# Moving six of seven fast-matrix products of a down-projection in between the blocks of the up-projection

## The chip, the cores and the metric

The kernel runs as one program on one core of a Trainium2 chip. The metric is the device time of one execution in microseconds (us); the time of a kernel is the median of several executions. The core has a matrix engine (TensorE, PE in the profile, with its weight loads shown as PEld), a vector engine (VectorE, DVE), a scalar engine (ScalarE, ACT), a general engine (GpSimd, POOL) and a queue engine (SyncE, SP) that here issues DMA transfers. Results of TensorE go to eight accumulator banks of 128 x 512 floats.

## The reference

A two-layer encoder over 256 tokens of width 2048. Each layer is a token mixer (a state-space mixer, then windowed attention) followed by the MLP below, each with a normalisation in front and a residual add behind. Both layers' MLPs are the place of the change:

```
D_MODEL, SEQ, D_FF = 2048, 256, 8192

def sqrelu_mlp(h, w_up, w_down):
    return jnp.square(jax.nn.relu(h @ w_up)) @ w_down

h = h + sqrelu_mlp(rms_norm(h, mlp_norm[i]), mlp_w_up[i], mlp_w_down[i])
```

All inputs and outputs are float32.

## The kernel before

**Matmuls in split precision.** A float32 matrix is split into a high part, which is its value cast to the reduced float32 format that TensorE takes at full rate, and a low part, the difference. A product of two matrices is then three matmuls: high by high, low by high, high by low. ScalarE makes the high part (a cast, lines 679 and 693 for weights, 917 for activations), VectorE the low one (a subtraction, lines 680, 694 and 918).

**Weights.** `wload` (line 665) takes the next source from the list `wsrc`, issues one transfer of 128 x 2048 floats on SP's queue into the next buffer of the ring of raw weights, and makes the high and low part in the next buffers of two more rings. `wnext` (line 710) keeps one block loaded ahead of the one that it hands out. While the MLP runs, the raw ring has two buffers and the high and low rings three each; the down-projection adds one to each for a part of its time. The engines' orders are made by a scheduler at build time from the order in which the program is written and the dependencies; each engine then runs its list in order, and the ring buffers decide how far the loads run ahead.

**Up-projection.** The 8192 hidden features are computed in 64 blocks of 128 (`up_mm`, line 856). A block is 16 matmuls of 512 columns with the high weights (line 858; the right side holds the activations' high and low parts side by side) and 16 of 256 columns with the low weights (line 860), into one bank. `up_post` (line 862) empties the bank: ScalarE copies one half (865), VectorE adds the other (866) and applies the relu and the row scale (867), ScalarE squares (869) into the hidden array `hT`. It is written behind the next block's matmuls. The up-projection uses the eight banks in turn.

**Down-projection.** It makes two passes (`half`), one per 1024 output columns. A pass goes over 32 k-pairs; a pair is two blocks of 128 hidden features, so 256 rows of the weight. The output of a pass is a 2 x 2 grid of banks (`x1` to `x4`: two token halves by two column halves), and a pair is a 2 x 2 by 2 x 2 block product. `plain` (line 938) computes it as 8 block products, `fast` (line 934) as 7 by Winograd's form of Strassen's scheme, from sums and differences of activation and weight blocks. The seven products go to `p1`, `x1`, `x2`, `q5`, `q6`, `q7`, `x3`; the four banks p1 and q5 to q7 collect over all fast pairs of the pass and are combined and added to the residual by `fold` (line 948). The first pass has nine fast pairs (2, 5, ... 26), the second nine others:

```
FORMS = (("p1", 0, 0, 1), ("x1", 1, 0, 2), ("x2", 6, 0, 0), ("q5", 4, 1, 0),
         ("q6", 5, 1, 1), ("q7", 3, 1, 2), ("x3", 2, 1, 3))   # bank, activation form, weight set, weight block
```

`wload_fast` (line 683) makes the weights of a fast pair: it splits three of the four raw blocks (1536 columns, first set), forms three differences in place (lines 696 to 698) and splits all four (2048 columns, second set). `split` (line 902) does the activations of a pair, one pair ahead of the matmuls: for a plain pair a cast and a subtraction of 512 columns, for a fast one also a copy and the sums of lines 912 to 914 and 896 columns.

`end` (line 960) adds the x banks to the residual. Between the two MLPs lies the attention layer, in front of the first the state-space layer; neither is touched but for scratch memory. On-chip memory is handed out by an arena with fixed boundaries (line 189), where a range keeps one number format until all its tenants are freed.

## Time and profile before

| | |
|---|---|
| time, median of 3 runs (lowest to highest) | 2065.54 us (2063.76 to 2065.96) |
| profiled execution: its own time | 2068.43 us |
| profiled execution: span from first to last instruction | 2066.6 us |
| mean granted TensorE clock | 0.996 |
| transferred | 368.47 MB, mean 178 GB/s |
| MLP 1: up-projection, down-projection | about 385 to 747 us, 747 to 1092 us |
| MLP 2: up-projection, down-projection | about 1380 to 1722 us, 1722 to 2064 us |

How to read the rows shown below: an L number is a line of the kernel before; `x` is a count of instructions; a group's row gives its summed busy time, the mean duration of one in ns, and behind the bar the idle time of the engine just ahead of these instructions with the instruction that ended it (behind the arrow). `slot` is a range of on-chip memory, `bank` an accumulator bank, `in_wdn` the down-projection's weights. Matmuls overlap in the pipe, so the mean duration of one is longer than the time from one to the next.

### The profile page before, as it was taken

What the parts mean: (1) busy time and instruction counts of PE and PEld (TensorE: products, weight loads), DVE (VectorE), ACT (ScalarE), POOL (GpSimd) and SP (SyncE); (2) the same over time, 40 slices, a digit from 0 to 9 for tenths busy, and PEclk for the clock granted to TensorE, in tenths of its full rate; (3) what the DMA queues carried; (4) which work ended last, traced back from release to release, by engine and by line L of the source; (5) the groups of instructions that cost most, each with busy time, mean ns of one, the idle gap of its engine ahead of it and who ended that gap; (6) DMA issues with size and microseconds to landing.
All of it is one profiled execution on the core that took longest, in us unless ns stands there. A gap on an engine that the chain in (4) does not pass through costs nothing.

```text
span 2066.6 us, 33166 instructions
## 1 busy us (share of the span) xinstructions
PE 2002.8 (97%) x13736; PEld 1685.1 (82%) x13736; DVE 1478.7 (72%) x2184; ACT 1091.4 (53%) x1320; POOL 246.7 (12%) x218
## 2 busy tenths in 40 slices
PE   4989999999999999999999999999999999999999
PEld 4877778888888887878788867888888888887887
DVE  8889736765555568888887877565555557888886
ACT  6553555454444455565654666444444445565553
POOL 6987730000000000000010000000000000000000
PEclk9999999999999999999999999999999999999999
DMA  3234456465555555565565432555555555557554
GB/s 121 69 97 141 155 176 230 144 222 184 185 196 190 184 182 203 215 215 195 212 210 183 139 118 86 189 184 185 193 192 184 188 196 201 190 185 242 186 207 157
DMA packets 61990, 368.47 MB, mean 178 GB/s; under 512 B 7072, under 2 KB 9408, under 8 KB 21904
## 3 DMA queue, kind: packets, MB, share of 16 engines
q1 hardware_dynamic: 54144, 342.32, 47.2%
q10 hardware_dynamic: 5184, 19.49, 2.9%
q0 software_dynamic: 2512, 4.56, 1.2%
q8 instruction: 107, 1.75, 0.3%
q14 instruction: 43, 0.35, 0.0%
HBM read 360.05 MB, written 2.10 MB: 175 GB/s over the span
## 4 chain that ended last, share of the span: by engine, by line
PE 69%; DVE 7%; DMA 5%; ACT 2%; issue 2%; DVEq 0%; ACTq 0%
PE bank L858 23%; PE bank L924 20%; PE bank L860 12%; DMA slot<-in_wdn 4%; PE bank L717 4%; PE bank L719 4%; PE bank L718 4%; DVE slot L680 3%; DVE slot L694 1%; ACT slot L693 1%; DVE slot L918 1%; ACT slot L1149 1%; PE bank L1169 1%; PE bank L1160 1%; PE bank L1130 1%
## 5 line engine op out<-in xcount | busy, mean ns | idle before, releaser
L680 DVE TENSOR_TENSOR slot<-slot,slot 128x2048 fp32r<-128x2048 f32 (+1 forms) x295 | 639.1, 2169 | 411.1 <-ACT slot L679 409.0
L679 ACT CAST slot<-slot 128x2048 fp32r<-128x2048 f32 (+1 forms) x319 | 554.6, 1743 | 455.7 <-PE bank L858 188.8
L924 PE MATMUL bank<-slot,slot 128*128 128x512 f32 x2124 | 493.7, 390 | 2.0 <-DVE slot L918 1.4
L858 PE MATMUL bank<-slot,slot 128*128 128x512 f32 x2048 | 491.8, 392 | 0.1
L924 PEld LDWEIGHTS bank<-slot,slot 128*128 128x128 f32 x2124 | 397.7, 188 | 88.3 <-DVE slot L918 4.5
L858 PEld LDWEIGHTS bank<-slot,slot 128*128 128x128 f32 x2048 | 377.1, 189 | 73.3 <-DVE ms L755 0.3
L860 PEld LDWEIGHTS bank<-slot,slot 128*128 128x128 f32 x2048 | 263.1, 191 | 10.3
L860 PE MATMUL bank<-slot,slot 128*128 128x256 f32 x2048 | 266.3, 283 | 0.0
L717 PE MATMUL bank<-slot,slot 128*128 128x512 f32 x544 | 216.5, 399 | 3.8 <-ACT slot L1174 2.0
L718 PE MATMUL bank<-slot,slot 128*128 128x512 f32 x544 | 213.6, 393 | 0.0
L719 PE MATMUL bank<-slot,slot 128*128 128x512 f32 x544 | 208.7, 395 | 4.7 <-POOL slot L680 4.5
L924 PE MATMUL bank<-slot 128*128 128x512 f32 x840 | 201.3, 391 | 5.8 <-DVE slot L918 5.1
L924 PEld LDWEIGHTS bank<-slot 128*128 128x128 f32 x840 | 156.9, 188 | 42.1 <-DVE slot L918 8.2
L951 POOL DMA_DIRECT2D slot<-slot x4 | 3.7, 914 | 1490.7 <-ACT slot L950 1490.7
L693 ACT CAST slot<-slot 128x1536 fp32r<-128x1536 f32 x72 | 122.3, 1698 | 98.5 <-DMA slot<-in_wdn 49.1
L694 DVE TENSOR_TENSOR slot<-slot,slot 128x1536 fp32r<-128x1536 f32 x72 | 145.6, 2022 | 39.2 <-ACT slot L693 36.5
L869 ACT ACTIVATE slot<-slot 128x256 f32<-128x256 f32 x128 | 52.8, 414 | 151.7 <-DVE slot L867 151.7
L717 PEld LDWEIGHTS bank<-slot,slot 128*128 128x128 f32 x544 | 102.4, 188 | 27.9 <-ACT slot L679 2.5
L719 PEld LDWEIGHTS bank<-slot,slot 128*128 128x128 f32 x544 | 102.2, 189 | 27.8 <-POOL slot L680 5.4
L718 PEld LDWEIGHTS bank<-slot,slot 128*128 128x128 f32 x544 | 102.6, 189 | 20.7 <-issue 0.8
L917 ACT CAST slot<-slot 128x512 fp32r<-128x512 f32 (+1 forms) x128 | 90.7, 710 | 52.1 <-PE bank L924 51.4
L918 DVE TENSOR_TENSOR slot<-slot,slot 128x512 fp32r<-128x512 f32 (+1 forms) x128 | 101.8, 798 | 1.3 <-ACT slot L917 0.7
(237 smaller groups left out, 1698.8 us busy)
## 6 DMA issues: line engine op xcount, KB each, us to landing
slot<-in_wup SPq DMA_DIRECT2D x128, 1024.0 KB, 4.9
slot<-in_wdn SPq DMA_DIRECT2D x128, 1024.0 KB, 5.0
slot<-in_wqkv SPq DMA_DIRECT2D x20, 1024.0 KB, 4.9
slot<-in_wge ACTq DMA_DIRECT2D x32, 512.0 KB, 4.0
slot<-in_wgl SPq DMA_DIRECT2D x16, 1024.0 KB, 5.0
slot<-in_wo SPq DMA_DIRECT2D x16, 1024.0 KB, 4.9
slot<-in_bz SPq DMA_DIRECT2D x16, 336.0 KB, 3.3
slot<-in_cp SPq DMA_DIRECT2D x16, 256.0 KB, 2.7
```

Source lines behind the costliest of these rows:

```text
L679: self.nc.scalar.copy(hi[:, c], raw[:, c])
L680: (self.nc.gpsimd if e == "g" else self.nc.vector).tensor_sub(lo[:, c], raw[:, c], hi[:, c].bitcast(F32))
L693: self.nc.scalar.copy(hi, x)
L694: v.tensor_sub(lo, x, hi.bitcast(F32))
L717: pe.matmul(out, lhsT=xh, rhs=wh, start=first, stop=False)
L718: pe.matmul(out, lhsT=xl, rhs=wh, start=False, stop=False)
L719: self.dm = pe.matmul(out, lhsT=xh, rhs=wl, start=False, stop=last)
L858: pe.matmul(bk, lhsT=wh[:, kt], rhs=act[:, kt].rearrange("p x c -> p (x c)"), start=(kt == 0), stop=False)
L860: pe.matmul(bk[:, :L], lhsT=wl[:, kt], rhs=act[:, kt, 0], start=False, stop=(kt == KT - 1))
L917: nc.scalar.copy(a[:, :c], h)
L918: v.tensor_sub(a[:, n:n + c], h, a[:, :c].bitcast(F32))
L924: pe.matmul(bank(bk), lhsT=a[x][:, j], rhs=w[y][:, c], start=bk not in begun, stop=stop and y == 1)
```

## The change

In each MLP, 24 of the first pass's 32 k-pairs (0 to 23) are computed while the up-projection is still running, each some blocks after its hidden features exist.

- Behind up block `fb` for the 24 blocks in `SIX` (6, 8, 10, 13, 15, 17, 20, ... 59), six of the seven products of one pair are issued (`SIXTH`), into the banks p1, x2, q5, q6, q7 and x3, which stay open from block 6 on. Six banks are thus held and two are left for the up blocks.
- Their weights follow the up block's weights in the load list. `wload_fast` with six forms splits 1024 columns for the first set, makes the same three differences, and splits 2048 for the second. Their activations are made by `split6` in one buffer (`asix`): a cast and a subtraction of 256 columns, three sums, a cast and a subtraction of 512.
- The seventh product (x1, an untransformed weight block times an untransformed activation block) is left to the pass, four pairs to an item: six items of 12 matmuls, whose weight blocks lie together in a new array `wp2` (six loads of 128 x 2048 per MLP more).
- The first pass is then these six items and the eight plain pairs 24 to 31, in the order of `PASS`. The second pass is as it was. The seven-product pairs of the first pass are gone.
- `fold0` adds the four combined banks to the residual in place on VectorE in the pass's third item; before, `fold` did it with accumulating transfers on GpSimd's queue.
- Activations in the passes are split two items ahead, from four narrow buffers in the first pass, and one wide and two narrow in the second.
- Buffers: from block 2 on the raw ring has three more (two of them until block 45) and the high and low ring one more each (until block 29); in the pass the high and low rings get one more again, the raw ring one more from the third item on. The hidden array's second and third part get their memory at blocks 33 and 49. The scratch of the normalisation is closed during the up-projection, and the arena has one more boundary.
- The first pair's casts and differences may not be issued ahead of block 1's evacuation (`gate`).

The diff, cut to its core:

```diff
-WD = 20 + 16 + 64 + 64
-FAST = (range(2, 27, 3), (0, 4, 7, 10, 13, 16, 20, 23, 26))
+SIX = {6 + 7 * p // 3: p for p in range(24)}
+FAST = (0, 4, 7, 10, 13, 16, 20, 23, 26)
+PASS = ((-1, 24, -2, 25, 26, -3, 27, -4, 28, 29, -5, 30, -6, 31), range(32))
 QH = ("v", "vv", "vv", "v") + ("vv", "v") * 8
 UH = ("vv", "vv", "vv", "vv", "vv")
-OH = ("v",) * 16
...
+    def add(self, *more):
+        for t in more:
+            self.i = max(self.i, 0)
+            self.tiles.insert(self.i, t)
+            self.i += 1
+
+    def drop(self, *more):
+        for t in more:
+            i = [x is t for x in self.tiles].index(True)
+            self.i -= i <= self.i
+            del self.tiles[i]
...
     def wload(self):
         if self.wsrc:
-            src = self.wsrc.pop(0)
-            if src is None:
+            if self.wsrc[0] is None:
+                self.wsrc.pop(0)
                 self.wring(D)
-                src = self.wsrc.pop(0)
-            if len(self.wsrc) in self.wfast:
-                return self.wload_fast(src)
+            src, how = self.wsrc.pop(0)
+            if how in (6, 7):
+                return self.wload_fast(src, how)
             raw, hi, lo = (r.next() for r in self.wr)
             (self.nc.scalar if raw.shape[1] < D else self.nc.sync).dma_start(raw, src)
-            how = self.whow.get(len(self.wsrc), "v")
             m = raw.shape[1] // len(how)
             for i, e in enumerate(how):
...
-    def wload_fast(self, src):
+    def wload_fast(self, src, forms):
...
         pair = raw[:, 1024:].rearrange("p (x c) -> p x c", x=2)
         out = []
-        for x, n in (raw[:, 512:], 1536), (raw, 2048):
+        for x in raw[:, 512:1536 if forms == 6 else 2048], raw:
+            n = x.shape[1]
             hi, lo = (r.next()[:, :n] for r in self.wr[1:])
             self.nc.scalar.copy(hi, x)
             v.tensor_sub(lo, x, hi.bitcast(F32))
...
-        hTs = [ar.get("hT#%d" % i, [n, L], at=o) for i, (n, o) in enumerate(((32, 31744), (16, 39936), (16, 44032)))]
+        hTs = [ar.get("hT#0", [32, L], at=31744)]
...
+            m = nc.scalar.copy(t, bk[:, L:]), nc.vector.tensor_add(s, bk[:, :L], t)
...
+            return m
...
-            up_post(fb, early[fb][0])
...
+        self.tmp.close()
+        atail = []
+        asix = ar.get("w6", [1536], F32R, at=4096)
+        ssix = ar.get("s6", [512], at=51712)
+        wraw, whi, wlo = self.wr
+
+        def extra(at, dt=F32):
+            return ar.get("wx#%d" % at, [2048], dt, at=at)
+        raw3, raw45 = extra(49664), [extra(at) for at in (44032, 46080)]
+        wraw.add(raw3, *raw45)
+        more = [extra(at, F32R) for at in (39936, 41984)]
+        whi.add(more[0])
+        wlo.add(more[1])
+
...
+        def halves(a, h, n):
+            c = int(np.prod(h.shape[1:]))
+            o = a[:, :c], a[:, n:n + c]
+            if len(h.shape) > 2:
+                o = [x.rearrange("p (x c) -> p x c", x=h.shape[1]) for x in o]
+            nc.scalar.copy(o[0], h)
+            v.tensor_sub(o[1], h, o[0].bitcast(F32))
+            return a[:, :n], a[:, n:]
+
+        def sums(t, q):
+            v.tensor_add(t[:, 0:2], q[:, 1:4:2], q[:, 0:1].broadcast_to([P, 2, P]))
+            v.tensor_add(t[:, 2], t[:, 1], q[:, 1])
+            v.tensor_add(t[:, 3], t[:, 2], q[:, 2])
+
+        def split6(kp):
+            q = hpair(kp).rearrange("p (x c) -> p x c", x=4)
+            halves(asix, q[:, 1:4:2], 768)
+            sums(ssix.rearrange("p (x c) -> p x c", x=4), q)
+            halves(asix[:, 256:], ssix, 768)
+            return asix[:, :768], asix[:, 768:]
+
+        def split(kp, a, fast):
             n = a.shape[1] // 2
+            if kp < 0:
...
+                h = hTs[0][:, 8 * k + 1:8 * k + 8:2, :P] if k < 4 else hTs[1][:, 8 * k - 31:8 * k - 24:2, :P]
+                return halves(a, h, n)
...
             if fast:
                 s = pool.tile([P, 7 * P], F32, name="sr", bufs=1)
...
+                sums(s.rearrange("p (x c) -> p x c", x=7)[:, 3:], h.rearrange("p (x c) -> p x c", x=4))
                 h = s
...
+            return halves(a, h, n)
...
+        SIXTH = (("p1", 0, 0, 1), ("x2", 5, 0, 0), ("q5", 3, 1, 0), ("q6", 4, 1, 1), ("q7", 2, 1, 2), ("x3", 1, 1, 3))
+
+        def fast(a, w, forms, end):
+            for bk, j, g, c in forms:
                 mm(bk, a, j, w[g], c, stop=end and bk[0] != "x")
...
+        def fold0():
+            p1, q5, q6, q7 = (bks[n] for n in ("p1", "q5", "q6", "q7"))
+            v.tensor_add(rs(0, 0), rs(0, 0), p1)
+            nc.scalar.copy(ssix, p1)
+            v.tensor_sub(ssix, ssix, q6)
+            v.tensor_add(rs(0, 1), rs(0, 1), ssix)
+            v.tensor_sub(rs(0, 1), rs(0, 1), q5)
+            v.tensor_sub(ssix, q7, ssix)
+            v.tensor_add(rs(1, 0), rs(1, 0), ssix)
+            v.tensor_add(ssix, ssix, q5)
+            v.tensor_add(rs(1, 1), rs(1, 1), ssix)
+
         def fold():
-            c, d, u, w = (self.tmp.tile([P, 512], F32, name=n) for n in ("hg", "hg", "sq", "gain"))
+            f = ar.get("fo", [4, 512], at=37888)
+            c, d, u, w = (f[:, i] for i in range(4))
...
+        bks, begun = {}, set()
+        six = None
+        for fb in range(2, FF // P):
+            with ExitStack() as gate:
+                if fb == min(SIX):
+                    for m in begin:
+                        gate.enter_context(self.tc.issue_after(m.ins))
+                wh, wl = wup()
+            bk = self.bank()
+            up_mm(bk, wh, wl, range(KT))
+            if fb == 29:
+                whi.drop(more[0])
+                wlo.drop(more[1])
+            if fb == 45:
+                wraw.drop(*raw45)
+            if fb in (33, 49):
+                at = 39936 if fb == 33 else 44032
+                ar.free("wx#%d" % at, "wx#%d" % (at + 2048))
+                hTs.append(ar.get("hT#%d" % len(hTs), [16, L], at=at))
+            if post:
+                up_post(*post)
+            post = (fb, bk)
+            if fb + 1 in SIX:
+                six = split6(SIX[fb + 1])
+            if fb in SIX:
+                fast(six, self.wnext(), SIXTH, fb == max(SIX))
+        ar.free("w6")
+        atail += [ar.get("at#%d" % i, [1024], F32R, at=4096 + 1024 * i) for i in range(2)]
+        ready = [split(PASS[0][i], atail[i], False) for i in range(2)]
         w0 = self.wnext()
         up_post(*post)
         ar.free("act", "ml.up")
         del pool.rings["up"]
-        aform += [ar.get("af#%d" % i, [2048], F32R, at=27648 + 2048 * i) for i in range(2)]
-        for r, at in zip(self.wr[1:], (23552, 25600)):
-            r.add(ar.get("wx#%d" % at, [2048], F32R, at=at))
+        aform = Ring([ar.get("af#%d" % i, [1024], F32R, at=27648 + 1024 * i) for i in range(4)])
+        more = [extra(at, F32R) for at in (23552, 25600)]
+        whi.add(more[0])
+        wlo.add(more[1])
         for half in range(2):
-            bks, begun = {}, set()
+            if half:
...
-            for kp in range(NK):
-                a = nx
-                if half == 0 and kp == 2:
+            items = PASS[half]
+            for i, kp in enumerate(items):
+                a = ready.pop(0)
+                if half == 0 and i == 2:
                     ar.free("at")
-                    self.wr[0].add(ar.get("wx#49664", [2048], at=49664))
-                if half and kp == NK - 4:
-                    for r in self.wr:
-                        r.drop()
+                    raw4 = extra(4096)
+                    wraw.add(raw4)
+                    self.tmp = Scope(ar, "tm", 2, 4096)
+                if half and i == NK - 4:
+                    wraw.drop(raw3, raw4)
+                    whi.drop(more[0])
+                    wlo.drop(more[1])
                     ar.free("wx")
-                    atail[:] = [ar.get("at#%d" % i, [1024], F32R, at=49664 + 1024 * i) for i in range(2)]
-                if kp + 1 < NK:
-                    nx = split(kp + 1, kp + 1 in FAST[half], kp == 0 if not half else kp + 1 >= NK - 2)
-                elif not half:
-                    nx = split(0, 0 in FAST[1])
-                w = self.wnext() if half or kp else w0
+                    atail[:] = [ar.get("at#%d" % j, [1024], F32R, at=49664 + 1024 * j) for j in range(2)]
+                w = self.wnext() if half or i else w0
+                if half == 0 and i == 2:
+                    fold0()
+                    ar.free("s6")
+                if half and kp == 19:
...
-                if kp in FAST[half]:
-                    fast(a, w, not begun, kp == FAST[half][-1])
-                    if kp == FAST[half][-1]:
+                if kp < 0:
+                    for j in range(4):
+                        mm("x1", a, j, w, j)
+                elif half and kp in FAST:
+                    fast(a, w, FORMS if begun else LATE, kp == FAST[-1])
+                    if kp == FAST[-1]:
                         fold()
                 elif kp < NK - 1 - half:
                     for b in range(4):
                         plain(a, w, b)
                 else:
                     pend.append((a, w))
+                k = (*items, *PASS[1])[i + 2] if not half or i + 2 < NK else None
+                if half or i + 2 >= len(items):
+                    if len(aform.tiles) == 4:
+                        ar.free("af")
+                        wide, aform = ar.get("aw", [2048], F32R, at=27648), ar.ring("af", 2, [1024], F32R, at=29696)
+                    if k is not None:
+                        f = k in FAST
+                        ready.append(split(k, atail[i % 2] if half and i >= NK - 4 else wide if f else aform.next(), f))
+                else:
+                    ready.append(split(k, aform.next(), False))
...
-        self.wfast = {n - 1 - 32 * h - kp for n in (64, 64 + WD) for h in range(2) for kp in FAST[h]}
+        def mlp(l):
+            for b in range(64):
+                yield d["wup"][l, b], UH[b] if b < len(UH) and not l else "v"
+                if b in SIX:
+                    yield d["wdn"][l, SIX[b]], 6
+            for half in range(2):
+                for kp in PASS[half]:
+                    yield (d["wp2"][l, -1 - kp], "v") if kp < 0 else (d["wdn"][l, 32 * half + kp], 7 if half and kp in FAST else "v")
...
-        n = len(self.wsrc)
-        self.whow.update({n - i: "g" for i in WP})
+        for i in WP:
+            if self.wsrc[i - 1]:
+                self.wsrc[i - 1][1] = "g"
...
+    w = mlp_w_down.reshape(2, FF // P // 2, 2, P, D)[:, :len(SIX), 1, :, :512]
+    r["wp2"] = c(w.reshape(2, len(SIX) // 4, 4, P, 512).transpose(0, 1, 3, 2, 4)).reshape(2, len(SIX) // 4, P, D)
```

60 lines of the change are left out of this document (18 added, 42 removed).

## The prediction

> **What bounds the kernel now.** I read the busy table first, then the stages around the two MLPs, then who made TensorE wait, then the price of each kind of instruction.
>
> The page's busy table, and the answer that cuts the span into stages (columns: length, then busy time and instructions of PE, PEld, DVE, ACT, POOL, granted clock, DMA share, GB/s). The rows are MLP 1's up-projection, MLP 1's down-projection, MLP 2's up-projection, MLP 2's down-projection:
>
> ```profile
> span 2066.6 us, 33166 instructions
> PE 2002.8 (97%) x13736; PEld 1685.1 (82%) x13736; DVE 1478.7 (72%) x2184; ACT 1091.4 (53%) x1320; POOL 246.7 (12%) x218
> 385.00:747.00 362.00, 359.29 (x2058) 317.09 (x2057) 205.98 (x231) 170.42 (x203) 0.00 (x0) 1.00 0.54 185
> 747.00:1092.00 345.00, 340.51 (x1495) 278.38 (x1495) 294.62 (x310) 200.18 (x181) 9.89 (x13) 1.00 0.59 205
> 1380.00:1722.00 342.00, 342.00 (x1970) 302.38 (x1970) 191.06 (x191) 162.50 (x191) 0.00 (x0) 1.00 0.55 193
> 1722.00:2064.00 342.00, 337.38 (x1479) 276.41 (x1477) 282.90 (x267) 190.50 (x160) 6.95 (x8) 1.00 0.57 196
> ```
>
> TensorE is busy in nearly every microsecond of all four stages (342.00 of 342.00 in MLP 2's up-projection) at full granted clock. VectorE is 56% busy in the up-projections and 83 to 85% in the down-projections. So a matmul taken away shortens the end, if whatever replaces it fits beside what is left.
>
> What TensorE waited for in the two down-projections, and in the first half of MLP 2's (columns: total us, times, longest), with the two waits of MLP 1's first half from the timeline:
>
> ```profile
> PE bank L924 <- DVE slot L918: 3.4, 5, 1.1
> PE bank L924 <- ACT slot L917: 0.7, 1, 0.7
> PE bank L924 <- DVE slot L918: 3.1, 4, 1.3
> PE bank L924 <- DVE slot L918: 1.5, 2, 0.9
> 798.16 2.11 PE L924 MATMUL bank<-slot 128*128 128x512 f32 x8 [1.10 <-DVE slot L918]
> 904.28 10.27 PE L924 MATMUL bank<-slot,slot 128*128 128x512 f32 x44 [1.04 <-DVE slot L918]
> ```
>
> The waits come to 3.4 + 0.7 + 3.1 = 7.2 us in both MLPs, all for the activation split (lines 917 and 918), never for a weight or a bank. The first halves hold 1.10 + 1.04 + 1.5 = 3.6 us of them.
>
> **What a matmul and an up block cost.** From the chain of waits (start, length):
>
> ```profile
> 736.82 3.65 PE bank L858 x16
> 742.39 3.65 PE bank L858 x16
> 798.16 82.89 PE bank L924 x364
> ```
>
> An up block repeats every 742.39 - 736.82 = 5.57 us; 364 down-projection matmuls without a stall took 82.89 us, or 0.2277 us each.
>
> The Trainium skill (TensorE: Matmul & The Clock Gate, Back-to-back issue gap) gives 216 ns for an isolated 512-column matmul and about 131 ns for a sustained stream with weight loads; 90 matmuls would be 19.4 or 11.8 us by these. The trace's 228 ns stands against the second.
>
> **The matmuls removed.** In the first pass a plain k-pair takes 8 products of 3 matmuls, a fast one 7 of 3. Before: 23 x 24 + 9 x 21 = 741. After: 24 pairs of 18 between up blocks (432), six x1 items of 12 (72), eight plain pairs (192): 696. That is 45 fewer per MLP, 90 in all: 90 x 0.2277 = **20.5 us less**. The second pass keeps its 741.
>
> **The work that moves under the up blocks.** The cost is VectorE's. Its and ScalarE's prices (the last two numbers before the bar's idle time are busy us and mean ns):
>
> ```profile
> L680 DVE TENSOR_TENSOR slot<-slot,slot 128x2048 fp32r<-128x2048 f32 x257 | 588.2, 2290 | 397.5 <-ACT slot L679 397.3
> L918 DVE TENSOR_TENSOR slot<-slot,slot 128x512 fp32r<-128x512 f32 x92 | 62.8, 686 | 1.3 <-ACT slot L917 0.7
> L867 DVE SCALAR_TENSOR_TENSOR slot<-slot 128x256 f32<-128x256 f32 x128 | 54.3, 425 | 4.1
> L866 DVE TENSOR_TENSOR slot<-bank,slot 128x256 f32<-128x256 f32 x128 | 53.4, 417 | 1.2 <-ACT slot L869 1.2
> L698 DVE TENSOR_TENSOR slot<-slot 128x1024 f32<-128x1024 f32 x36 | 44.1, 1224 | 1.0
> L697 DVE TENSOR_TENSOR slot<-slot 128x512 f32<-128x512 f32 x36 | 24.8, 689 | 0.7
> L912 DVE TENSOR_TENSOR slot<-slot 128x256 f32<-128x256 f32 x36 | 15.1, 420 | 0.3
> L914 DVE TENSOR_TENSOR slot<-slot,slot 128x128 f32<-128x128 f32 x36 | 10.3, 286 | 0.1
> L679 ACT CAST slot<-slot 128x2048 fp32r<-128x2048 f32 x257 | 491.0, 1911 | 402.2 <-PE bank L858 180.0 <-PE bank L924 93.0 <-PE bank L718 31.8
> L679 ACT CAST slot<-slot 128x1024 fp32r<-128x1024 f32 x62 | 63.9, 1050 | 53.5 <-PE bank L718 14.0 <-PE bank L858 8.8 <-DVE slot L543 8.1
> L917 ACT CAST slot<-slot 128x512 fp32r<-128x512 f32 x92 | 56.8, 620 | 51.7 <-PE bank L924 51.4
> L869 ACT ACTIVATE slot<-slot 128x256 f32<-128x256 f32 x128 | 52.8, 414 | 151.7 <-DVE slot L867 151.7
> L865 ACT COPY slot<-bank 128x256 f32<-128x256 f32 x128 | 46.7, 365 | 11.0 <-PE bank L860 7.3 <-ACT slot L679 0.3
> ```
>
> An up block costs VectorE 2.290 + 0.417 + 0.425 = 3.13 us. A six-product pair costs it, for weights, 1.224 (low part of the 1024-wide form, priced as line 698's equal size) + 0.689 + 0.689 + 1.224 + 2.290 = 6.12, and for activations 0.420 (a 256-wide subtraction) + 0.420 + 2 x 0.286 + 0.686 = 2.10: 8.22 us.
>
> Three pairs go with seven up blocks. TensorE needs 7 x 5.57 + 3 x 18 x 0.2277 = 51.3 us for them, VectorE 7 x 3.13 + 3 x 8.22 = 46.6 us (91%), ScalarE 7 x (1.911 + 0.365 + 0.414) + 3 x (1.050 + 1.911 + 0.365 + 0.620) = 30.7 us (60%). TensorE stays the longest by 4.7 us a cycle. Where only two blocks lie between pairs it is 15.2 against 14.5 us.
>
> Does a load of that height run without stopping TensorE? The middle of MLP 1's first pass, where one fast pair in three has a similar load, says yes:
>
> ```profile
> 840.00:860.00 20.00, 20.00 (x89) 16.52 (x88) 18.40 (x18) 11.93 (x11) 0.00 (x0) 1.00 0.63 227
> 860.00:880.00 20.00, 20.00 (x90) 16.56 (x89) 16.84 (x18) 11.64 (x10) 0.00 (x0) 1.00 0.65 241
> 880.00:900.00 20.00, 20.00 (x90) 16.57 (x89) 18.88 (x17) 12.87 (x11) 2.33 (x3) 1.00 0.66 209
> ```
>
> VectorE is busy 54.1 of 60 us (90%), TensorE 60 of 60. There are four high and four low weight buffers there; the change has four until block 29, three after. So I lay out the tight two-block interval with three, from one up block's timeline:
>
> ```profile
> 501.15 1.91 ACT L679 CAST slot<-slot 128x2048 fp32r<-128x2048 f32 x1 [3.22 <-PE bank L858]
> 503.12 2.29 DVE L680 TENSOR_TENSOR slot<-slot,slot 128x2048 fp32r<-128x2048 f32 x1 [2.48 <-ACT slot L679]
> 508.43 3.82 PE L858 MATMUL bank<-slot,slot 128*128 128x512 f32 x16
> 510.89 0.42 DVE L866 TENSOR_TENSOR slot<-bank,slot 128x256 f32<-128x256 f32 x1
> ```
>
> Call the start of the block in front of a pair 0. Its high buffer is free at 3.65 and its low one at 5.57; the pair runs from 5.57 to 9.67, the next blocks from 9.67 and 15.23, the next pair from 20.8. VectorE can then do the low part of the block at 9.67 by 8.1, an evacuation by 8.9, the low part of the next block from 9.0 to 11.3, the next pair's first form and transforms to 15.2, its activation work to 17.3 (ScalarE's cast beside it), its second form to 19.6, another evacuation to 20.4; the next buffer frees at 20.8. Nothing is late: the second form is due at about 22.2 (the first six matmuls read the other), so a delay of 2.6 us is absorbed, and a three-block interval gives 3.2 us back. The single activation buffer is free from 9.67 to 20.8, against a chain of 3.1 us on both engines.
>
> New waits on TensorE I bound by the old ones: from none, to the mean of the five above (0.68 us) at each of 48 pairs, 33 us. With those deadlines I am near the low end: 4 us, one pair in eight. The first halves' 3.6 us of old waits go with the fast pairs that made them.
>
> **The rest, at nothing.** The pass that remains has TensorE 264 x 0.2277 = 60.1 us and VectorE 14 x (2.290 + 0.686) = 41.7 us, plus the new fold of eight 512-wide operations (5.5 us). The fold's banks aren't wanted before the second pass; uncovered it would cost 11 us in both MLPs. An x1 item (2.73 us on TensorE, 2.98 on VectorE) always stands beside a plain pair of 5.46. ScalarE's added casts and copies lie in its 40% of free time. Six loads are added per MLP on SP's queue:
>
> ```profile
> slot<-in_wdn SPq DMA_DIRECT2D x128, 1024.0 KB, 5.0
> ```
>
> Ten loads of 1.05 MB a cycle are 205 GB/s; fourteen in the pass are 244 GB/s, against 241 moved in the row at 860; at 241 the pass would take 0.8 us more. The gate on the first pair puts its casts and differences behind block 1's evacuation, early in MLP time, with nobody waiting. Ring additions, freed scratch and the finer arena touch buffers whose readers are done; splitting activations two items ahead can only ease the second pass's waits.
>
> **Sum.** Against the profiled execution's 2068.43 us: 2068.4 - 20.5 + 4 - 3.6 = 2048.3. That execution lies 2.9 us above the median of 2065.54, so the median to expect is 2045.4; I say **2046**, with 2040 to 2053 as this case's own range.
>
> **Rivals.**
> *VectorE paces the up blocks a little.* At the 10% idle share of the 60 us above, a cycle takes 46.6 / 0.902 = 51.7 us, 0.4 too long in each of 16 cycles: 6.5 us, so 2052; with somewhat more idle, up to 2064. For it: the load is 91%. Against it: that idle was slack, as TensorE never waited.
>
> *VectorE becomes the bound, slower than before.* The 503.12 row shows VectorE idle for 2.48 us in front of the low part, because the cast waits for the buffer's last matmul. Idle time it can't fill decides from 4.7 us a cycle, and the gain is gone at 4.7 + 20.5/16 = 6.0. One such gap per pair is 3 x 2.48 = 7.4 us: (7.4 - 4.7) x 16 = 43 us, or 2065.5 - 20.5 + 43 = 2088. Against it: the gap exists while VectorE has nothing else, and the pairs bring it work. The Trainium skill (Perfetto Trace Analysis, Optimization Strategy) reads a gap that repeats as too few buffers; the 2.48 us agrees, and the change later has no more of these buffers.
>
> *Two banks.* Six banks are held, so block n's evacuation must end before block n+2 starts. At 508.43 a block ends, and its sum is done at 511.31, 2.9 us later of 5.57 allowed. With a first form and transforms ahead of it (3.8 us) it is 1.1 us late; at 16 of the 64 places with no pair between, 18 us: 2063. Against it: the evacuation is written ahead of the next pair's load.
>
> *All old waits vanish, none come:* 2065.5 - 20.5 - 7.2 = 2038.
>
> *The change doesn't do what it says* (TensorE wasn't the bound): 2066. The up stage's 342.00 of 342.00 excludes it nearly.
>
> **How the numbers follow.** Forecast 0.65, VectorE pacing a little 0.14, VectorE the bound 0.09, two banks 0.05, no waits 0.06, no effect 0.01. This kernel's measurement tells about 0.2% (4.1 us) from no change. Below 2061.4: 0.65 + 0.06 + 0.10 of the pacing + 0.01 of the banks = 0.82; above 2069.7: the bound's 0.09 and 0.01 of the others = 0.10; between, 0.08. The range 2039 to 2064 leaves out the slower cases and part of the fastest.
>
> **What would show it.** Right: TensorE's matmuls fall by 90 to 13646 and its busy time by some 20 us; the up stages' stretches between blocks 6 and 59 take 51.3 us a cycle with VectorE near 90% and TensorE without repeating waits; the pass takes about 60 us. Wrong: waits of TensorE in the up stage for lines of the weight differences (VectorE the bound), for the evacuation's reads (banks), or for the new activation split; or a granted clock under 1.00.

## The result, and the profile after

The changed kernel takes 2043.45 us (median; 2042.0 to 2045.99) against 2065.75 us in the same comparison: ratio 0.9894, 95% interval 0.9876 to 0.9911. That is 22.3 us less; 2046 was forecast, with 2039 to 2064 as the range. The two profiled executions differ by 24.4 us in span (2066.6 to 2042.2), and that difference is followed here. The ratios below leave out two executions far slower than the others of their kernel: one of the kernel before (2840.11 us) and one of the run with plain pairs (4047.79 us).

The page's busy table of the changed kernel:

```profile
span 2042.2 us, 33455 instructions
PE 1979.6 (97%) x13646; PEld 1671.3 (82%) x13646; DVE 1632.5 (80%) x2474; ACT 1140.9 (56%) x1404; POOL 239.5 (12%) x210
```

TensorE has 90 matmuls and 23.2 us of busy time less, VectorE 154 us more.

Where TensorE works, by its lines (count, shortest, median and longest duration in ns, first and last start in us): first of the kernel before, the high-weight (line 858) and low-weight (860) matmuls of MLP 1's up-projection and the down-projection (924) behind it, then the same three of MLP 2.

```profile
L858 PE MATMUL bank<-slot,slot x1024: 387/389/628, 385.7 to 745.7; 128*128 128x512 f32 x171
L860 PE MATMUL bank<-slot,slot x1024: 277/283/285, 388.4 to 747.7; 128*128 128x256 f32 x171
L924 PE MATMUL bank<-slot,slot x1062: 387/389/504, 747.8 to 1092.5; 128*128 128x512 f32 x177
...
L858 PE MATMUL bank<-slot,slot x1024: 387/389/499, 1362.9 to 1718.8; 128*128 128x512 f32 x171
L860 PE MATMUL bank<-slot,slot x1024: 277/283/283, 1368.8 to 1720.8; 128*128 128x256 f32 x171
L924 PE MATMUL bank<-slot,slot x1062: 387/389/499, 1721.0 to 2062.3; 128*128 128x512 f32 x177
```

The same of the changed kernel, where the lines are 862, 864 and 953; line 953 now starts inside the up-projection:

```profile
L862 PE MATMUL bank<-slot,slot x1024: 387/389/775, 389.7 to 849.9; 128*128 128x512 f32 x171
L864 PE MATMUL bank<-slot,slot x1024: 277/283/283, 392.4 to 852.0; 128*128 128x256 f32 x171
L953 PE MATMUL bank<-slot,slot x1266: 387/389/476, 436.9 to 1080.6; 128*128 128x512 f32 x181
...
L862 PE MATMUL bank<-slot,slot x1024: 387/389/501, 1354.5 to 1808.4; 128*128 128x512 f32 x171
L864 PE MATMUL bank<-slot,slot x1024: 277/283/283, 1360.4 to 1810.4; 128*128 128x256 f32 x171
L953 PE MATMUL bank<-slot,slot x1266: 388/389/398, 1395.3 to 2038.2; 128*128 128x512 f32 x181
```

The up-projection's end is taken as the last start of the low-weight matmuls. From these starts, in us:

| stretch | before | after | difference | matmuls alone |
|---|---|---|---|---|
| to MLP 1's first matmul | 385.7 | 389.7 | +4.0 | 0 |
| MLP 1 up (after: with 24 pairs) | 362.0 | 462.3 | +100.3 | +97.9 |
| MLP 1 down, both passes | 344.8 | 228.6 | -116.2 | -108.1 |
| attention, to MLP 2's first matmul | 270.4 | 273.9 | +3.5 | 0 |
| MLP 2 up | 357.9 | 455.9 | +98.0 | +97.9 |
| MLP 2 down | 341.5 | 227.8 | -113.7 | -108.1 |
| tail | 4.3 | 4.0 | -0.3 | 0 |

The last column takes 0.2267 us a matmul, from the longest stretch of the changed kernel's chain of waits: 933 of them in 211.51 us.

```profile
636.28 3.65 PE bank L862 x16
641.84 4.11 PE bank L953 x18
645.95 3.63 PE bank L862 x16
651.49 3.65 PE bank L862 x16
...
852.24 211.51 PE bank L953 x933
```

A moved pair takes 4.11 us and the blocks keep their 5.55 us, one straight behind the other. Stage by stage, the same view as before the change (columns: length, busy and instructions of PE, PEld, DVE, ACT, POOL, clock, DMA share, GB/s): three cycles of seven blocks and three pairs, the first pass with part of the second, and the rest of the second.

```profile
437.00:488.20 51.20, 51.20 (x280) 44.57 (x279) 43.51 (x51) 29.51 (x34) 0.00 (x0) 1.00 0.57 204
488.20:539.40 51.20, 51.20 (x280) 44.57 (x279) 43.51 (x51) 29.54 (x34) 0.00 (x0) 1.00 0.57 206
...
693.00:744.30 51.30, 51.30 (x280) 44.65 (x279) 42.71 (x50) 29.26 (x35) 0.00 (x0) 1.00 0.46 162
...
852.20:920.00 67.80, 67.80 (x301) 56.12 (x300) 55.20 (x49) 43.88 (x46) 0.00 (x0) 1.00 0.70 250
920.00:1083.00 163.00, 163.00 (x729) 135.07 (x728) 139.57 (x165) 91.10 (x85) 6.48 (x9) 1.00 0.57 198
```

TensorE is busy for the whole of each stretch. A cycle takes 51.2 to 51.3 us; VectorE is busy for 43.5 us of the first two and 42.7 of the third. TensorE's waits between the first block and the end of MLP 1 are down to one, in the normalisation (line 748 is line 744 of before); in MLP 2 there is none:

```profile
PE bank L748 <- DVE slot L739: 4.7, 1, 4.7
```

So the difference of 24.4 us is made of 20.4 us of matmuls (90 x 0.2267), 13.7 us of stalls in the passes that are gone (8.1 and 5.6, the differences beyond the last column), less about 10 us that came back elsewhere: 4.0 ahead of MLP 1, 2.4 in MLP 1's up-projection, 3.5 in attention.

The 13.7 us are more than the 7.2 us of waits that the prediction counted, though the waits it counted were all. The waits of the weight loads show why, in MLP 1's down-projection of before:

```profile
PEld bank L924 <- DVE slot L918: 6.9, 8, 1.5
PEld bank L924 <- ACT slot L917: 1.1, 1, 1.1
PEld bank L924 <- DVE slot L680: 0.5, 1, 0.5
PEld bank L924 <- ACT slot L693: 0.5, 1, 0.5
```

They come to 9.0 us, close to the stage's 344.8 - 1482 x 0.2267 = 8.8 us over its matmuls, where the matmuls' own rows have 4.1. In MLP 2's down-projection it is 6.6 us by the weight loads and 3.1 by the matmuls, for 5.5 us lost. Part of the gap is in the records: one matmul's lasts 0.389 us while the next follows after 0.2267, so idle time counted from the end of a record misses up to 0.16 us of each wait. The rest of the gap stays open.

By passes (the second begins with its first matmul, found by count): before 172.2 and 172.6 us in MLP 1, 171.0 and 170.4 in MLP 2, against 168.0 for 741 matmuls; after 60.0 and 168.7, 60.0 and 167.7. Both passes lost their stalls, the second too, though its work is unchanged. What did that was the first question for the runs.

### The profile page after: what moved, and what is told of

Read it like the earlier page. It is cut to its first block, busy times and chain, and to the rows that moved or that the text cites. A ratio compares the mean times of both kernels' runs of the same rounds, so it can differ in the third digit from the quotient of the medians.

```text
span 2042.2 us, 33455 instructions
## 1 busy us (share of the span) xinstructions
PE 1979.6 (97%) x13646; PEld 1671.3 (82%) x13646; DVE 1632.5 (80%) x2474; ACT 1140.9 (56%) x1404; POOL 239.5 (12%) x210
## 4 chain that ended last, share of the span: by engine, by line
PE 82%; POOL 6%; DVE 5%; ACT 3%; DMA 2%; issue 1%; ACTq 0%; SPq 0%; POOLq 0%; DVEq 0%
PE bank L953 32%; PE bank L862 23%; PE bank L864 12%; PE bank L721 4%; PE bank L723 4%; PE bank L722 4%; POOL slot L564 2%; DVE slot L683 1%; ACT slot L1239 1%; POOL slot L565 1%; POOL slot L505 1%; DMA slot<-in_wge 1%; PE bank L586 1%; PE bank L650 1%; ACT slot L682 1%
## 5 line engine op out<-in xcount | busy, mean ns | idle before, releaser
L683 DVE TENSOR_TENSOR slot<-slot,slot 128x2048 fp32r<-128x2048 f32 (+1 forms) x277 | 597.4, 2161 | 229.5 <-ACT slot L682 222.6
L682 ACT CAST slot<-slot 128x2048 fp32r<-128x2048 f32 (+1 forms) x301 | 519.7, 1734 | 373.5 <-PE bank L953 96.7
L953 PE MATMUL bank<-slot,slot 128*128 128x512 f32 x2532 | 591.3, 390 | 0.0
L953 PEld LDWEIGHTS bank<-slot,slot 128*128 128x128 f32 x2532 | 472.0, 188 | 95.8
L862 PE MATMUL bank<-slot,slot 128*128 128x512 f32 x2048 | 492.7, 391 | 0.1
L862 PEld LDWEIGHTS bank<-slot,slot 128*128 128x128 f32 x2048 | 380.3, 189 | 75.9 <-DVE ms L759 0.3
L698 DVE TENSOR_TENSOR slot<-slot,slot 128x2048 fp32r<-128x2048 f32 (+2 forms) x132 | 241.2, 1827 | 41.1 <-ACT slot L697 40.3
L864 PEld LDWEIGHTS bank<-slot,slot 128*128 128x128 f32 x2048 | 263.1, 191 | 10.3
L697 ACT CAST slot<-slot 128x2048 fp32r<-128x2048 f32 (+2 forms) x132 | 203.2, 1540 | 65.8 <-DVE slot L702 48.1
L721 PE MATMUL bank<-slot,slot 128*128 128x512 f32 x544 | 217.1, 400 | 6.1 <-ACT slot L1264 3.1
L722 PE MATMUL bank<-slot,slot 128*128 128x512 f32 x544 | 213.7, 393 | 0.0
L723 PE MATMUL bank<-slot,slot 128*128 128x512 f32 x544 | 207.8, 395 | 4.7 <-POOL slot L683 4.3
L920 ACT CAST slot<-slot 128x512 fp32r<-128x512 f32 (+2 forms) x188 | 108.1, 593 | 58.2 <-PE bank L953 37.3
L721 PEld LDWEIGHTS bank<-slot,slot 128*128 128x128 f32 x544 | 102.7, 189 | 30.9 <-ACT slot L682 3.7
L723 PEld LDWEIGHTS bank<-slot,slot 128*128 128x128 f32 x544 | 102.1, 189 | 28.5 <-POOL slot L683 5.2
L722 PEld LDWEIGHTS bank<-slot,slot 128*128 128x128 f32 x544 | 102.8, 189 | 21.1 <-issue 1.2
L921 DVE TENSOR_TENSOR slot<-slot,slot 128x512 fp32r<-128x512 f32 (+2 forms) x188 | 118.6, 655 | 0.8 <-ACT slot L920 0.8
L869 ACT COPY slot<-bank 128x256 f32<-128x256 f32 x128 | 47.4, 370 | 121.3 <-PE bank L864 120.7
```

The source lines that it names most:

```text
L682: self.nc.scalar.copy(hi[:, c], raw[:, c])
L683: (self.nc.gpsimd if e == "g" else self.nc.vector).tensor_sub(lo[:, c], raw[:, c], hi[:, c].bitcast(F32))
L697: self.nc.scalar.copy(hi, x)
L698: v.tensor_sub(lo, x, hi.bitcast(F32))
L721: pe.matmul(out, lhsT=xh, rhs=wh, start=first, stop=False)
L722: pe.matmul(out, lhsT=xl, rhs=wh, start=False, stop=False)
```

## The experiments

The ratios are to the kernel before in the same comparison (its median there was 2067.3 to 2068.2 us); the changed kernel has 0.9894. Stage times are those of the one profiled execution of each run.

**A split two ahead, in the kernel before.** In both passes the activations are split two items ahead, from one wide and two narrow buffers:

```diff
-        aform += [ar.get("af#%d" % i, [2048], F32R, at=27648 + 2048 * i) for i in range(2)]
+        wide, aform = ar.get("af#w", [2048], F32R, at=27648), ar.ring("af", 2, [1024], F32R, at=29696)
...
+                if not half or kp + 2 < NK:
+                    k, f = (kp + 2) % NK, (kp + 2) % NK in FAST[half + (kp + 2) // NK]
+                    ready.append(split(k, f, atail[kp % 2] if half and kp >= NK - 4 else wide if f else aform.next()))
```

> The kernel before, with one thing changed: the activations of both passes are split two items ahead (one wide buffer for fast pairs, two narrow ones for plain pairs, in the same memory). Theory A (the passes' stalls come from the split standing one item ahead): both down-projections take close to their 1482 matmuls at 0.2267 us, 336 to 337 us each, instead of 344.5 and 341.3; no wait of TensorE for the activation split; total 2052 to 2055 us. Theory B (they came from the fast pairs' load in the first pass and the smaller rings): the down-projections stay at 341 to 345 us, total 2064 to 2067 us.

2143.47 us, ratio 1.0369 (1.0352 to 1.0385): 75 us slower, which neither theory had. The two down-projections take 380.1 and 378.8 us, and TensorE waits all over them, mostly for the split (here lines 917, VectorE, and 916, ScalarE), less for the casts of weights (679):

```profile
PE bank L923 <- DVE slot L917: 29.6, 15, 4.0
PE bank L923 <- ACT slot L916: 8.9, 8, 3.1
PE bank L923 <- ACT slot L679: 6.6, 2, 3.5
```

Theory A falls: a longer lead, with the activation buffers that go with it and three raw buffers, does harm. The lead and the shape of the buffers changed together here.

**The memory layout, in the kernel before.**

```diff
-        self.ar = Arena(self.const, [0, 7168, 13312, ...
+        self.ar = Arena(self.const, [0, 4096, 7168, 13312, ...
...
+        for n in ("hg", "sq", "gain"):
+            self.tmp.reserve(n, 512)
```

> The kernel before, with only the arena's new boundary at 4096 and the scratch reserved at the start of the attention layer. Theory A (the 10 us that the changed kernel loses outside its passes come from this memory layout): the state-space stage is about 4 us longer and the attention stage about 3.5 us, total 2070 to 2075 us. Theory B (they come from scatter between executions and from the order of work that meets the new up-projection): total 2064 to 2068 us.

2069.12 us, ratio 1.0001 (0.999 to 1.0012); the time lies between the two theories' ranges, as the kernel before itself had 2068.15 in this comparison. Its profiled execution is 1.4 us later at MLP 1 and 1.5 us longer in attention, which the times don't show. Theory B by the ratio: the layout doesn't cost the 10 us, though a cost of up to 2.5 us lies inside the interval.

**One ahead, in the changed kernel.**

```diff
-                k = (*items, *PASS[1])[i + 2] if not half or i + 2 < NK else None
+                k = (*items, *PASS[1])[i + 1] if not half or i + 1 < NK else None
```

(with this split written ahead of the item's matmuls, as before the change)

> The changed kernel, with the activations of the passes split one item ahead, as before the change. Theory A (two items ahead removed the second pass's stalls): waits of TensorE for the activation split come back in the second passes, 2 to 4 us in each MLP, total 2047 to 2052 us. Theory B (the rings and the lighter first pass did it): no waits, total 2042 to 2046 us.

2044.51 us, ratio 0.989 (0.9875 to 0.9906), down-projections at 228.6 and 227.8 us, no wait in them. Theory B: in the changed kernel the second item of lead does nothing.

**Three high and three low buffers throughout.**

```diff
-        whi.add(more[0])
-        wlo.add(more[1])
...
-            if fb == 29:
-                whi.drop(more[0])
-                wlo.drop(more[1])
```

> The changed kernel, with three high and three low weight buffers through the whole up-projection instead of four until block 29. The timetable of the prediction: nothing is late with three, a cycle of seven blocks and three pairs stays at 51.2 to 51.3 us, total 2042 to 2046 us. The rival (too few buffers leave VectorE idle in front of each low part): waits of TensorE between blocks 6 and 29, up to 2.7 us a cycle for 3.4 cycles and two MLPs, total up to 2062 us.

2040.58 us, ratio 0.9872 (0.9854 to 0.9889), 2.9 us below the changed kernel's median, though the intervals overlap. No wait between blocks 6 and 29, so the timetable of the prediction holds. MLP 1's up-projection takes 460.0 us instead of 462.3, 98.0 more than before, where the matmuls alone make 97.9: the 2.4 us lost there came with the fourth buffer. The normalisation's products, which wait for VectorE at that place, wait 2.7 us again instead of 4.7:

```profile
PE bank L748 <- DVE slot L739: 2.7, 1, 2.7
```

The other runs agree: this wait is 4.7 us in those with the fourth buffer (one ahead, three raw, plain pairs, more VectorE work) and 2.7 with 28 pairs and three buffers. VectorE's timeline shows what slips ahead. In front of the products of line 739 the changed kernel makes the low part of a 2048-wide block beside a 1024-wide one, the run with three buffers only a 1024-wide one:

```profile
391.63 3.42 DVE L683 TENSOR_TENSOR slot<-slot,slot 128x2048 fp32r<-128x2048 f32 x2
392.29 1.22 DVE L683 TENSOR_TENSOR slot<-slot,slot 128x1024 fp32r<-128x1024 f32 x1
```

**Three raw buffers in the passes of the changed kernel.**

```diff
-                    wraw.add(raw4)
```

> The changed kernel without the raw ring's fourth buffer in the passes (three, as before the change). Theory A (the fourth raw buffer removed the second pass's stalls): they come back, 2 to 6 us in each MLP, with waits of TensorE for the activation split, total 2047 to 2056 us; if three buffers and a split two ahead go badly together, as in the kernel before with a split two ahead, up to 15 us in each. Theory B (the first pass without fast pairs did it, VectorE enters the second pass with nothing left over): no waits, both down-projections at 228 us, total 2042 to 2046 us.

2063.95 us, ratio 0.9984 (0.9974 to 0.9993): most of the gain is gone. The first passes stay at 60 us; the second ones take 180.9 and 176.4 us instead of 168.7 and 167.7. TensorE's timeline in MLP 1's second pass (the bracket is the idle time and who ended it):

```profile
996.31 0.50 PE L953 MATMUL bank<-slot,slot 128*128 128x512 f32 x1 [0.93 <-ACT slot L920]
997.68 10.53 PE L953 MATMUL bank<-slot,slot 128*128 128x512 f32 x44 [0.87 <-ACT slot L697]
...
1018.21 9.86 PE L953 MATMUL bank<-slot,slot 128*128 128x512 f32 x30 [2.92 <-ACT slot L682]
1077.13 15.73 PE L953 MATMUL bank<-slot,slot 128*128 128x512 f32 x68 [2.19 <-DVE slot L921]
```

The stalls are in the middle and at the end of the pass, and they end with casts of weights (lines 682 and 697) and splits (920, 921). Work of the next layer isn't needed for them: MLP 2, the last stage, has such stalls too, the longest 2.35 us at 1985.29. What the buffer does is seen in who waits for transfers: in MLP 2's second pass ScalarE and VectorE stand idle for `in_wdn` for 48.0 us in sum, in the changed kernel for 12.2.

**The same, one ahead:** the edits of this run and of the one-ahead run together.

> The changed kernel with three raw buffers in the passes and the activations split one item ahead: in the second pass the rings' depth and the split's lead are those before the change, what differs is the first pass ahead of it and the activation buffers. If a split two ahead needs the fourth raw buffer and one ahead does not (theory C), the second passes take 168 to 170 us, total 2042 to 2047 us. If the fourth raw buffer is needed with either (theory A), they take 176 to 181 us as without it and two ahead, total 2058 to 2064 us. If neither matters beyond what the kernel before shows, 170 to 173 us, total 2047 to 2051 us.

2063.49 us, ratio 0.9975 (0.9964 to 0.9986), second passes 182.9 and 178.3 us. Theory A for the changed kernel: without the fourth raw buffer 17 to 19 us are lost by the ratios, whatever the split's lead; the down-projections lose 20.9 and 24.7 us in the profiled executions.

**A fourth raw buffer in the kernel before**, with the first pass's banks added in place to free the memory:

```diff
+                    self.wr[0].xtra = [ar.get("wx#%d" % at, [2048], at=at) for at in (49664, 4096)]
...
-                        fold()
+                        fold() if half else fold0()
```

> The kernel before with a fourth raw buffer from the third pair of the first pass on, in the memory of the normalisation's scratch; to free it, the first pass's four banks are added to the residual in place, as the change does. Matmuls and their order are those of before. Theory A (the fourth raw buffer): down-projections at 336 to 338 us instead of 344.8 and 341.5, total 2053 to 2058 us. Theory B (the lighter first pass): 341 to 345 us, total 2064 to 2069 us.

2069.58 us, ratio 1.0007 (0.9997 to 1.0018), down-projections at 343.8 and 339.1 us. By itself the buffer does nothing in the total: MLP 2's second pass is at 168.3 us, but MLP 1's is at 173.9. It does shorten the waits of casts (lines 679 and 693) and weight differences (696) for transfers. Between 750 and 920 us, in MLP 1's first pass, they were 37.0 us in the kernel before (the first three rows; total us, times, longest) and are 3.1 here (the last two):

```profile
ACT slot L693 <- DMA slot<-in_wdn: 17.8, 8, 4.8
ACT slot L679 <- DMA slot<-in_wdn: 7.6, 4, 3.0
DVE slot L696 <- DMA slot<-in_wdn: 11.6, 9, 3.3
...
ACT slot L679 <- DMA slot<-in_wdn: 1.6, 2, 1.2
DVE slot L696 <- DMA slot<-in_wdn: 1.5, 3, 1.1
```

**Both in the kernel before:** fourth raw buffer and split two ahead.

> The kernel before with both: a fourth raw buffer in the passes and the activations split two ahead from one wide and two narrow buffers. The second pass then has the machinery of the changed kernel, the first pass is still that of before, with nine fast pairs. Theory D (the machinery as a whole frees the second pass): second passes at 168 to 169 us, no waits for the split, total 2050 to 2057 us. Theory B (the lighter first pass does it): second passes at 170 us or more, total 2060 us or more, up to the 2143 us of two ahead with three raw buffers.

2057.42 us, ratio 0.9952 (0.9935 to 0.9968). Down-projections at 337.9 and 336.9 us, second passes at 168.7 and 167.7, with every matmul of the kernel before. All that TensorE still waits for in both, in sum over the run:

```profile
PE bank L923 <- ACT slot L693: 0.9, 2, 0.4
```

Theory D: the passes' stalls go with the machinery of the passes as a whole (four raw buffers, the split two ahead from wide and narrow activation buffers), and need no lighter first pass. Of the two parts one alone gives nothing and the other alone costs 75 us.

This run is also the fair base for the idea itself, as it has the machinery without the moved pairs. It gains about 10 us by its ratio, so nearly half of the changed kernel's 22 us needs no moved pair. Against it the profiled execution of the changed kernel is 19.9 us shorter in the four MLP stages, close to the 20.4 us of 90 matmuls, and 6.2 us longer outside them.

**The scheme without the place:** 24 fast pairs in the first pass of the kernel before.

```diff
-FAST = (range(2, 27, 3), (0, 4, 7, 10, 13, 16, 20, 23, 26))
+FAST = (range(2, 26), (0, 4, 7, 10, 13, 16, 20, 23, 26))
```

> The kernel before with 24 fast pairs (2 to 25) in the first pass instead of nine and nothing moved: TensorE's matmuls are as few as in the changed kernel (13646). If the count of matmuls alone set the time, 2045 us. If VectorE sets the pass, a fast pair costs it 6.65 us for weights and 2.08 for activations and a plain one 2.98: 24 x 8.73 + 8 x 2.98 = 233 us for a pass in which TensorE has 158 us of work and which takes some 171 us now; about 60 us more in each MLP, total 2160 to 2190 us.

2234.3 us in the one execution that was timed, with the matmuls of the changed kernel: 167 us slower than before in the same comparison, and above the 2160 to 2190 us expected. The first passes take 256.6 and 253.0 us. In MLP 1's:

```profile
748.00:930.00 182.00, 128.96 (x459) 92.68 (x458) 167.48 (x186) 93.69 (x82) 0.00 (x0) 0.89 0.35 122
```

VectorE is busy 92% and TensorE 71%, at a granted clock of 0.89. Over the whole pass VectorE is busy for 226 of 256.6 us, so its work alone is far longer than TensorE's 158 us; the 30 us of idle on top were not in the expectation. So what the change moves is VectorE's work, from a pass without room into up blocks with 43 to 44% idle.

**The place without the scheme:** the 24 pairs computed plainly between the same blocks.

```diff
-                    yield d["wdn"][l, SIX[b]], 6
+                    yield d["wdn"][l, SIX[b]], "v"
...
-                fast(six, self.wnext(), SIXTH, fb == max(SIX))
+                w6 = self.wnext()
+                for b in range(4):
+                    plain(six, w6, b)
```

> The changed kernel with the 24 moved pairs computed plainly, eight products of three matmuls into x1 to x4, between the same up blocks; no six-product forms, no x1 items, no first fold; the pass has the eight plain pairs. The place without the scheme: 13790 matmuls, 144 more than the changed kernel and 54 more than before. If TensorE is the bound and the place costs nothing: 2043.5 + 144 x 0.2267 = 2076 us, which is 10 us above the kernel before, with no waits in the MLPs. If the place itself brings something beside the matmul count, it is below 2072 us; if the smaller VectorE load matters to the changed kernel, it is below 2076 by that.

2073.09 us, ratio 1.0025 (1.0016 to 1.0035), no wait in the passes. 144 matmuls more than the changed kernel are 32.6 us; the medians differ by 29.6 us, the ratios by some 27. In the four MLP stages of the profiled executions the difference is 32.5 us (65.2 more in the up-projections, 32.7 less in the down-projections); the rest lies outside the MLPs. The place brings nothing but room; the matmuls follow the count.

**More VectorE work per pair.** The low part of the 2048-wide form is made twice:

```diff
-            v.tensor_sub(lo, x, hi.bitcast(F32))
+            for _ in range(2 if forms == 6 and n == D else 1):
+                v.tensor_sub(lo, x, hi.bitcast(F32))
```

> The changed kernel with the low part of each moved pair's 2048-wide form made twice: one more VectorE instruction of 2.29 us for each of 48 pairs. By the prediction's sum VectorE would need 46.6 + 3 x 2.29 = 53.5 us a cycle against TensorE's 51.3: 2.2 us too long in 16 cycles, total about 2043.5 + 35 = 2079 us. By the busy time of the changed kernel's trace (43.5 us a cycle) it needs 50.4 us and still fits: total 2043 to 2050 us.

2089.98 us, ratio 1.0108 (1.0093 to 1.0123): 46.5 us above the changed kernel's median (44 by the ratios), more than either expectation had it. The up-projections take 24.8 and 25.5 us more. By cycles:

```profile
437.00:488.20 51.20, 51.20 (x280) 44.57 (x279) 47.89 (x53) 29.41 (x33) 0.00 (x0) 1.00 0.54 197
488.20:539.40 51.20, 51.20 (x280) 44.58 (x279) 48.78 (x55) 29.46 (x33) 0.00 (x0) 1.00 0.56 206
...
641.80:693.00 51.20, 48.19 (x259) 40.75 (x258) 46.28 (x52) 27.29 (x33) 0.00 (x0) 1.00 0.50 182
693.00:744.20 51.20, 48.74 (x253) 41.69 (x252) 44.52 (x51) 25.20 (x29) 0.00 (x0) 0.97 0.41 151
```

While there are four high and low buffers (to block 29, about 600 us) VectorE is busy up to 95% and TensorE doesn't stop. With three, VectorE is busy only 87 to 90% while TensorE loses 2.5 to 3 us a cycle in this view: VectorE has idle time of 5 us and more that it can't fill. That the smaller rings are the cause is read from where the stalls begin; a run of this load with four buffers throughout is missing. By busy time the load would have fitted (43.5 + 3 x 2.2 = 50.1 of 51.2 us). The changed kernel, with 7.7 us idle a cycle, is not far from that edge.

**Four pairs more.** Three buffers throughout, 28 pairs, one behind every second block; seven x1 items and four plain pairs in the pass:

```diff
-SIX = {6 + 7 * p // 3: p for p in range(24)}
+SIX = {6 + 2 * p: p for p in range(28)}
...
-PASS = ((-1, 24, -2, 25, 26, -3, 27, -4, 28, 29, -5, 30, -6, 31), range(32))
+PASS = ((-1, 28, -2, -3, 29, -4, -5, 30, -6, -7, 31), range(32))
```

> The changed kernel with three high and low weight buffers all through the up-projection and 28 pairs moved instead of 24, one behind every second block from 6 to 60; the first pass is then seven x1 items and four plain pairs. 24 matmuls fewer in both MLPs, 24 x 0.2267 = 5.4 us. If TensorE stays the bound: 2040.6 - 5.4 = 2035 us. If VectorE can't follow (two blocks and a pair cost it 14.5 us by the sum of durations, some 13.5 by busy time, against 15.2): a wait at many of 56 pairs, up to 1 us each, total up to 2090 us; the first pass, with 11 loads in 40.8 us, may wait for transfers, up to 4 us in each MLP.

2030.86 us, ratio 0.9816 (0.98 to 0.9831): faster than both kernels, by 37 us against the kernel before in the same comparison, clear of the changed kernel's interval, and 4 us below the 2035 expected. 24 matmuls account for 5.4 us of the 9.7 below the three-buffer run; up- and down-projections together are 7.2 us shorter, the rest lies outside the MLPs. TensorE has no wait in either MLP but the normalisation's 2.7 us. VectorE in MLP 1's and MLP 2's up-projection:

```profile
441.00:863.00 422.00, 422.00 (x2282) 366.82 (x2281) 371.54 (x440) 250.54 (x277) 0.00 (x0) 1.00 0.57 204
1365.00:1815.00 450.00, 450.00 (x2438) 391.38 (x2437) 393.95 (x472) 263.85 (x295) 0.00 (x0) 1.00 0.57 202
```

Busy 88% with TensorE at 100%, and three buffers. Here the pairs come two blocks apart everywhere; in the run with more VectorE work, at two, two and three blocks. Whether the spacing is what lets three buffers carry this load was not tested apart.

## Why the prediction was right, point by point

| term | predicted | measured |
|---|---|---|
| 90 matmuls | -20.5 | -20.4 |
| new waits at 48 pairs | +4 | 0 |
| old waits, first passes | -3.6 | -7.0 |
| second passes | 0 | -6.6 |
| MLP 1's up-projection, beside the pairs | 0 | +2.4 |
| ahead of MLP 1, and attention | 0 | +7.5 |
| sum (with the tail's -0.3) | -20.1 | -24.4 |

**The matmuls** came out to 0.1 us, and the two runs that change their number by the place or the scheme alone bear the mechanism out: the count pays where VectorE has room, and doesn't where it hasn't.

The total came nearer than its terms did, and that is luck: the waits came out 14.0 us better than the prediction had them, and 9.9 us were lost where it had nothing.

**VectorE's room** was judged rightly and its size wrongly: 46.6 us a cycle by durations, 43.5 by the trace. Neighbouring instructions overlap, as this row of before shows: two of 2.29 us in 4.49.

```profile
768.66 4.49 DVE L680 TENSOR_TENSOR slot<-slot,slot 128x2048 fp32r<-128x2048 f32 x2
```

In the changed kernel's first cycle 37 of 51 instructions begin before the one ahead has ended, by 0.083 us at the median; the durations still add up to 46.5 us, so the overlap is the whole difference of 3 us. The step that says three buffers are enough held in the run that has three from the start.

**The new waits** were priced at 4 us and are nothing; the deadlines of the timetable, from which I argued for the low end, kept all 48 pairs.

**The old waits** were mis-sized: 13.6 us went in both passes, against 7.2 us in the rows that I read and 3.6 us that I let go. The rows of the weight loads, 9.0 us in MLP 1 and 6.6 in MLP 2, had the size; I read only the matmuls'. They also name weights (lines 680 and 693, 0.5 us each in MLP 1), which the prediction said never caused a wait.

**The rest, at nothing** is the step that failed in its reasons. It had the ring additions as touching only buffers whose readers are done, and the lead of two items as what could ease the second pass. The runs show the reverse for the changed kernel: the lead does nothing there (and where the prediction had it as only able to help, it costs the kernel before 75 us with three raw buffers), and without the fourth raw buffer 17 to 19 of the 22 us are gone. The prediction named no such need. And the extra high and low buffers, put at nothing too, cost 2.4 us at MLP 1's start.

**The 7.5 us** outside the MLPs are not settled. The layout may be part of it: the three runs of the kernel before that have the new boundary reach MLP 1 at 387.1 to 387.7 us, the three without it at 385.3 to 386.0, so some 1.8 of the 4.0 us go with the layout, by one execution each. The runs that share this code have 387.7 to 390.6 us to MLP 1 and 269.9 to 273.9 us of attention, the runs with the MLPs of before 385.3 to 387.7 and 269.4 to 274.0, so that the attention's part lies within the spread of schedules.

**The rivals.** VectorE as the bound did not come true, but one more instruction a pair brings it about, and with it a likely place: three buffers and a load near 98%. Two banks: no wait for the evacuation in any run with two. No waits at all: true of the pairs and passes, and yet 2043 rather than 2038: 6.4 us more of old waits went than this rival counted, but 9.9 came back, 2.4 of them in MLP 1's up-projection and 7.5 outside the MLPs.

Why three raw buffers give second passes of 170 to 173 us in the kernel before, and 176 to 183 us in the changed one, stays open: activation buffers, first pass and schedule differ at once, and were not separated. So does which part of the wide and narrow buffers helps beside the fourth raw one.

## What to carry to other kernels

Count what a fast scheme saves on the bound engine, but look for the stretch in which the engine that pays for it has room; the same products cost 167 us in a full stage and took 20 us off in stages with 43 to 44% idle. A buffer ring that a change adds in passing is a term of its own: take it away in a run before crediting the idea, and try its depth and the lead of the work that uses it together, since each alone can do nothing or harm. In a stage with pipelined matmuls, read the waits of the weight loads beside those of the matmuls (not added to them), and check both against the stage's length less its matmuls.

## What the runs showed of the hardware that was not expected

A row of waits of the matmuls understates lost time: 4.1 us stood there for 8.8 us lost in MLP 1's down-projection, and the weight loads' rows had 9.0. The weight loads' rows aren't exact either: 71.9 us for 87.0 lost in the two down-projections of the kernel before with the split two ahead, where the matmuls' rows had 51.4.

VectorE's instructions overlap their neighbours by some 0.08 us, which took 3 us, or 6%, off the 46.5 us of durations in a cycle of 51 instructions.

Where TensorE paused often the granted clock fell too: 0.89 over 182 us of the pass with 24 fast pairs, against 1.00 in the stretches shown without waits. A few short waits did not do it: the down-projections of the kernel before had 1.00 with waits of up to 1.3 us.
